# A decoder layer on one core: 44 pairs of the second feed-forward take seven products from sums of weights made during the first feed-forward

## The chip, the cores and the metric

The kernel runs on one core of one Trainium2 chip. The metric is the device time of one execution in microseconds; the time before is the median of three executions, 2144.79 us (2144.66 to 2144.88). One execution was taken by the hardware profiler; it took 2145.35 us, and its traced span is 2143.6 us.

## The reference

One layer in float32 over 16 learned tokens and 256 tokens of 2048 numbers (272 rows): a gated feed-forward at half weight, a mixer (differential attention and a short convolution, gated and merged), a second gated feed-forward at half weight, and a last norm. Cut to what matters here:

```python
def swiglu_ffn(h, w_gu, w_down):
    gate, up = jnp.split(h @ w_gu, 2, axis=-1)
    return (jax.nn.silu(gate) * up) @ w_down

h = rms_norm(s, norm_ffn1[layer])
s = s + 0.5 * swiglu_ffn(h, ffn1_w_gu[layer], ffn1_w_down[layer])
...                                     # the mixer
h = rms_norm(s, norm_ffn2[layer])
s = s + 0.5 * swiglu_ffn(h, ffn2_w_gu[layer], ffn2_w_down[layer])
s = rms_norm(s, norm_final)
return s[:, N_META:]
```

`w_gu` is 2048 x 11264 and `w_down` 5632 x 2048 in both feed-forwards.

## The kernel before

**Numbers.** TensorE multiplies float32 as the sum of a high and a low part. Every weight that arrives from device memory (a tile `st` of up to 1 MB) is therefore split before use: ScalarE casts it to the high part `wh` (L325, L442), VectorE subtracts to get the low part `wl` (L330, L443), and TensorE does three matmuls for each product: high by high, low by high, high by low (L341 to L343, L536 to L538). `wh` and `wl` have three buffers each (`W_BUFS`), `st` has four (`ST_BUFS`). `st` is loaded on SyncE's (SP's) queue (L312, L558).

**First feed-forward** (L716 to L733; roughly the first 800 us). `linear` (L280) multiplies one column group of 512 weights by all 272 rows. It goes over the input in blocks of two chunks of 128 rows of weights: a cast, a subtraction and 2 x 4 x 3 matmuls of 128x272 for each block; one `st` holds two blocks. 11 groups have a gate and an up `linear` of 16 chunks; after six of them and again after the last five, four `linear`s of the down projection run. That is 528 chunks, in 265 blocks (the first chunks come singly). The results of one `linear` are evicted by VectorE and ScalarE during the next (L460 to L466, L193).

**Second feed-forward, gate and up** (`gate_up_mix`, L647; `linear_mix`, L516). 256 tokens and pairs of chunks. A pair forms a 2 x 2 block product of (gate, up) columns by two token halves. A pair of kind D does its eight products, 24 matmuls of 128x512. A pair of kind S does seven, 21 matmuls, from four sums of activations (`Mixed.combine`, L497) and four sums of weights: `t13` (two sums) and `t24` (two sums). The constants `FFN2_FIRST` (the first unit) and `FFN2` (the other ten units) write out the kinds of a unit's eight pairs and, for S, where the sums are made: by VectorE (L570 to L572), or `t13` by two DMAs of 512 KB on GpSimd's (POOL's) queue, the second accumulating (`prefetch`, L576; pairs in the fourth entry, `by_load`), with VectorE adding `t24` (L571, L572). The four blocks in an `st` of 1 MB are split in two tiles for D, and for S in four tiles: `st`'s third block, `st`'s first two, `t24`, `t13` (L596 to L601). `t24` has two buffers (tag `tt`); `t13` uses the three buffers of the pool `aux` (`N_AUX`), which also holds activation sums of other stages.

**What sets the order.** Each engine runs its instructions in one fixed order, and waits at any one of them whose operands are not there. The code is recorded in the order in which it is written; a scheduler then places the instructions on each engine, so a row can stand earlier or later than where the code writes it. The order of the built program is shown below for two engines.

Of the kernel before, what the change touches and what calls it, by code (L numbers as in the profile page):

```python
# [9 lines left out]
F32 = mybir.dt.float32  # L10
# [5 lines left out]
P = 128  # L16
D = 2048
# [3 lines left out]
F = 5632  # L21
# [34 lines left out]
AHEAD = 2  # L56
W_LAST = 8 * GC


@with_exitstack  # L60
def decoder_layer(ctx: ExitStack, tc: tile.TileContext, t, out):
# [5 lines left out]
    aux = ctx.enter_context(tc.tile_pool(name="aux", bufs=N_AUX))  # L67
    tmp = ctx.enter_context(tc.tile_pool(name="tmp", bufs=2))
    psum = ctx.enter_context(tc.tile_pool(name="ps", bufs=8, space=bass.MemoryType.PSUM))

# [192 lines left out]

    pending = []
    last_load, ahead_of_split = [], []
    side = []
# [9 lines left out]
    def drain():  # L276
        while ahead:
            ahead.pop(0)[0]()

    def linear(act, chunks, w, k0, t0, t1, name, evict, before=None, side_at=(5, 9, 13), after=None, later_at=LATER_AT):  # L280
# [11 lines left out]
        for b, b1 in zip(starts, starts[1:] + [len(chunks)]):  # L292
# [41 lines left out]
            for i, c in enumerate(blk):  # L334
                first, last = b + i == 0, b + i == len(chunks) - 1
                for j in range(GC):
                    a, f = acc[j][:, :n], slice(j * P, (j + 1) * P)
                    if 2 * n <= 512:
                        nc.tensor.matmul(acc[j][:, : 2 * n], wh[:, i, f], act.both(c, t0, t1), start=first, stop=False)
                    else:  # L340
                        nc.tensor.matmul(a, wh[:, i, f], act.part(c, 0, t0, t1), start=first, stop=False)  # L341
                        nc.tensor.matmul(a, wh[:, i, f], act.part(c, 1, t0, t1), start=False, stop=False)  # L342
# [131 lines left out]
    class Mixed:  # L474
# [14 lines left out]

        def sum_of_parts(self, p):  # L490
# [4 lines left out]
            self.combine(p, f)  # L495

# [18 lines left out]

    def linear_mix(plan, a, w, name, done, k0=0):  # L516

# [7 lines left out]
        kinds, turn_at, sums_at, by_load = plan  # L525
        nd, ns = kinds.count("D"), kinds.count("S")
        left = {k: 2 * nd * (k in "234x") + ns * (k != "x") for k in "1234567x"}
# [26 lines left out]
        def load(p):  # L554

            st = wpool.tile([P, 4, GW], F32, tag="st", bufs=ST_BUFS, name="st")
            n = 3 if p in by_load else 4
            nc.sync.dma_start(out=st[:, :n, :], in_=w[k0 // 2 + p, :, :n, :])  # L558
            if kinds[p] == "S":
                if not by_load:  # L560
# [19 lines left out]

        far = 2 if by_load else 1
        loaded = {k: load(k) for k in range(far)}
# [29 lines left out]

    def mixed(plan, a, w, name, end):

# [29 lines left out]

        linear_mix(plan, a, w, name, done)

    def gate_up_mix(plan, a, rtok, w_gu, g, m, gi):  # L647
# [11 lines left out]

        mixed(plan, a, w_gu[g], "pg", end)  # L660

# [596 lines left out]
def _laid_out(np, inputs):  # L1258
# [19 lines left out]
    d["w_out"] = np.stack([_in_pairs(np, a["w_out"][0], c, c + GW) for c in (0, W2)])  # L1278
    d["ffn2_w_gu"] = np.stack([_in_pairs(np, a["ffn2_w_gu"][0], c, F + c) for c in range(0, F, GW)])
    w = a["ffn2_w_down"][0]  # L1280
# [3 lines left out]
    return d  # L1284


# [16 lines left out]
```

## Time and profile before

| what | value |
|---|---|
| median of three executions | 2144.79 us |
| the profiled execution | 2145.35 us, span 2143.6 us |
| PE (TensorE) busy | 2132.6 us, 99% of the span |
| DVE (VectorE) busy | 1604.6 us, 75% |
| ACT (ScalarE) busy | 1105.6 us, 52% |
| POOL (GpSimd) busy | 62.6 us, 3% |
| read from device memory | 422.88 MB, 198 GB/s over the span |
| first feed-forward | to about 800 us of the span |
| second feed-forward | from about 1440 us to the end |

Busy times of PE are of pipelined matmuls: one lasts longer than the time until the next starts, and the time between starts is what a matmul costs. "Idle before, releaser" in a group's row tells how long an engine stood before such instructions and what ended that. A DMA's time "to landing" runs from its issue to its completion. Granted clock of TensorE: 0.999 over the span.

### The profile page before, as it was taken

The page shows a single profiled execution, that of the slowest core. Times are in us where ns is not written, and L with a number is a line of the kernel's source. Part 1 is how long each engine was busy: PE and PEld are TensorE (multiplying, and loading weights), DVE is VectorE, ACT ScalarE, POOL GpSimd, SP SyncE. Part 2 cuts the span into 40 slices and gives each one's busy share as a digit, 9 for nine tenths or more (in the row PEclk, how much of TensorE's full clock was granted, in tenths as well). Part 3 has the DMA queues.
Part 4 walks back from the last instruction along what each step waited for, and adds up shares of the span by engine and source line. Part 5 has one row for each costly group of instructions (what it writes and reads, how often), then busy time and mean ns, then how long its engine had stood idle before and what let it go on. Part 6 is the DMA issues. An engine that isn't in the chain of part 4 may idle for free.

```text
span 2143.6 us, 32626 instructions
## 1 busy us (share of the span) xinstructions
PE 2132.6 (99%) x13162; PEld 1925.8 (90%) x13162; DVE 1604.6 (75%) x2113; ACT 1105.6 (52%) x1391; POOL 62.6 (3%) x89
## 2 busy tenths in 40 slices
PE   9999999999999999999999999999999999999998
PEld 9999999999999998899988888888888888888887
DVE  7555554445555668867887889889999899988998
ACT  6444343344333455545555555557665566555665
POOL 0000000000000000000000000000000111001100
PEclk9999999999999999999999999999999999999999
DMA  7554555555545445544355555667876988669853
GB/s 276 179 177 177 179 179 177 177 177 177 177 177 178 177 177 196 182 167 144 138 196 196 197 197 183 214 207 235 252 249 193 276 261 272 216 218 299 261 199 138
DMA packets 69560, 431.29 MB, mean 201 GB/s; under 512 B 8480, under 2 KB 8736, under 8 KB 25888
## 3 DMA queue, kind: packets, MB, share of 16 engines
q1 hardware_dynamic: 57024, 389.72, 51.0%
q0 software_dynamic: 11808, 38.80, 8.3%
q8 instruction: 103, 1.69, 0.3%
q10 hardware_dynamic: 576, 0.67, 0.1%
q14 instruction: 49, 0.40, 0.1%
HBM read 422.88 MB, written 2.10 MB: 198 GB/s over the span
## 4 chain that ended last, share of the span: by engine, by line
PE 99%; DMA 0%; ACT 0%; DVE 0%; issue 0%; ACTq 0%
PE pg L538 6%; PE pg L536 6%; PE pg L537 6%; PE pd L343 4%; PE pg L341 4%; PE pg L342 4%; PE pg L343 4%; PE pd L341 4%; PE pu L343 4%; PE pu L341 4%; PE pu L342 4%; PE pd L342 4%; PE pd L538 4%; PE pd L536 4%; PE pd L537 4%; PE g L538 2%
## 5 line engine op out<-in xcount | busy, mean ns | idle before, releaser
L330 DVE TENSOR_TENSOR wl<-st,wh 128x1024 fp32r<-128x1024 f32 (+1 forms) x329 | 401.0, 1220 | 379.1 <-ACT wh L325 378.9
L325 ACT CAST wh<-st 128x1024 fp32r<-128x1024 f32 (+1 forms) x328 | 343.2, 1047 | 489.3 <-PE pu L342 150.7
L443 DVE TENSOR_TENSOR wl<-st,wh 128x1024 fp32r<-128x1024 f32 (+1 forms) x424 | 470.8, 1118 | 55.3 <-ACT wh L442 52.3
L442 ACT CAST wh<-st 128x1024 fp32r<-128x1024 f32 (+1 forms) x424 | 400.2, 970 | 209.0 <-PE pdx L537 60.4
L442 ACT CAST wh<-t 128x1024 fp32r<-128x1024 f32 x160 | 166.6, 1052 | 242.0 <-DVE t L572 158.9
L443 DVE TENSOR_TENSOR wl<-t,wh 128x1024 fp32r<-128x1024 f32 x160 | 193.8, 1222 | 56.9 <-ACT wh L442 52.3
L341 PE MATMUL pg<-h,wh 128*128 128x272 f32 x704 | 201.9, 288 | 1.6 <-ACT h L206 1.6
L343 PE MATMUL pd<-mh,wl 128*128 128x272 f32 x704 | 203.1, 288 | 0.0
L341 PE MATMUL pd<-mh,wh 128*128 128x272 f32 x704 | 202.2, 287 | 0.0
L341 PE MATMUL pu<-h,wh 128*128 128x272 f32 x704 | 201.9, 287 | 0.0
L342 PE MATMUL pg<-h,wh 128*128 128x272 f32 x704 | 201.8, 288 | 0.0
L343 PE MATMUL pu<-h,wl 128*128 128x272 f32 x704 | 201.7, 287 | 0.0
L342 PE MATMUL pu<-h,wh 128*128 128x272 f32 x704 | 201.7, 286 | 0.0
L342 PE MATMUL pd<-ml,wh 128*128 128x272 f32 x704 | 200.8, 285 | 0.0
L343 PE MATMUL pg<-h,wl 128*128 128x272 f32 x704 | 200.1, 288 | 0.0
L537 PE MATMUL pg<-wh,h 128*128 128x512 f32 x399 | 156.0, 391 | 0.0
L536 PE MATMUL pg<-wh,h 128*128 128x512 f32 x399 | 155.8, 390 | 0.0
L538 PE MATMUL pg<-wl,h 128*128 128x512 f32 x399 | 155.7, 391 | 0.0
L341 PEld LDWEIGHTS pg<-h,wh 128*128 128x128 f32 x704 | 133.1, 190 | 1.9 <-ACT h L206 1.9
L342 PEld LDWEIGHTS pd<-ml,wh 128*128 128x128 f32 x704 | 133.5, 190 | 0.0
L342 PEld LDWEIGHTS pg<-h,wh 128*128 128x128 f32 x704 | 133.1, 190 | 0.0
L342 PEld LDWEIGHTS pu<-h,wh 128*128 128x128 f32 x704 | 132.6, 188 | 0.0
(379 smaller groups left out, 4801.2 us busy)
## 6 DMA issues: line engine op xcount, KB each, us to landing
st<-in_ffn_w_gu_dram SPq DMA_DIRECT2D x140, 1024.0 KB, 4.8
st<-in_ffn_w_down_dram SPq DMA_DIRECT2D x82, 1024.0 KB, 4.8
st<-in_w_in_dram SPq DMA_DIRECT2D x32, 1024.0 KB, 4.8
st<-in_w_gate_dram SPq DMA_DIRECT2D x32, 1024.0 KB, 4.8
t<-in_ffn_w_gu_dram POOLq DMA_DIRECT2D x64, 512.0 KB, 6.7
st<-in_ffn_w_gu_dram SPq DMA_DIRECT2D x32, 768.0 KB, 6.2
st<-in_w_qb_dram SPq DMA_DIRECT2D x16, 1024.0 KB, 4.8
st<-in_w_branch_dram SPq DMA_DIRECT2D x16, 1024.0 KB, 4.8
```

The costliest lines, as they stand in the source:

```text
L325: nc.scalar.copy(out=wh[:, :m, :], in_=sw)
L330: nc.vector.tensor_sub(wl[:, :m, :], sw, wh[:, :m, :].bitcast(F32))
L341: nc.tensor.matmul(a, wh[:, i, f], act.part(c, 0, t0, t1), start=first, stop=False)
L342: nc.tensor.matmul(a, wh[:, i, f], act.part(c, 1, t0, t1), start=False, stop=False)
L343: nc.tensor.matmul(a, wl[:, i, f], act.part(c, 0, t0, t1), start=False, stop=last)
L442: part_last[:] = [nc.scalar.copy(out=wh, in_=src).ins]
L443: part_last.append(nc.vector.tensor_sub(wl, src, wh.bitcast(F32)).ins)
L536: nc.tensor.matmul(ps[k], hi, wh, start=first, stop=False)
L537: nc.tensor.matmul(ps[k], lo, wh, start=False, stop=False)
L538: nc.tensor.matmul(ps[k], hi, wl, start=False, stop=left[k] == 0)
```

## The change

In the second feed-forward a new kind of pair, P, does seven products like S, but its four sums of weights come ready from device memory: `load` brings three blocks of `st` (768 KB), then `t24` and `t13` (512 KB each), all on SP's queue. The first unit goes from five D and three S to four D and four P, the other ten units from four D and four S to three D, four P and one S. So 44 pairs are of kind P, and each of the 11 units has one pair more with seven products. The S that is left has its sums from VectorE; `prefetch` is not used any more.

The sums for P are made by `Making` during the first feed-forward, in 88 halves of 512 KB. Each is a fetch on POOL's queue into a tile `mk` of the pool `aux`, three VectorE adds in place (of 512, 256 and 256 numbers a partition), and a store on POOL's queue into a tensor in device memory, whose pieces are 1 KB long. `tick` is called after each chunk of a `linear` and writes, every fifth time (`TICKS`), the adds and the store of the half two places back (`MAKE_AHEAD`) and the fetch of a new one. The host also lays the blocks of these 44 pairs out a second time (`ffn2_made_of`), without arithmetic. One more sum of activations is made before the second feed-forward.

```diff
-FFN2_FIRST = ("DDDDSSDS", (1,), {(3, 0): 4, (3, 1): 5, (6, 0): 7}, (4, 5))
-FFN2 = ("DDSDSSDS", (1,), {(1, 1): 2, (3, 0): 4, (3, 1): 5, (6, 0): 7}, (2, 4, 5))
+FFN2_FIRST = ("DDDPDPPP", (1,), {}, ())
+FFN2 = ("DDPPDSPP", (1,), {(4, 1): 5}, ())
...
+TICKS = 5
+MAKE_AHEAD = 2
...
+        def fetch(self):
+            self.t = aux.tile([P, 4, GW // 2], F32, tag="act", name="mk")
+            nc.gpsimd.dma_start(out=self.t, in_=t["ffn2_made_of"][self.n, self.k])
+
+        def add(self):
+            v = self.t
+            nc.vector.tensor_add(v[:, 0:2, :], v[:, 0:2, :], v[:, 1:3, :])
+            nc.vector.tensor_add(v[:, 2, :], v[:, 2, :], v[:, 0, :])
+            nc.vector.tensor_add(v[:, 3, :], v[:, 3, :], v[:, 2, :])
+
+        def store(self):
+            if not self.k:
+                made[self.u][self.p] = kept.tile([P, 4, GW], F32, name=f"made{self.u}_{self.p}")
+            cs = slice(self.k * GW // 2, (self.k + 1) * GW // 2)
+            nc.gpsimd.dma_start(out=made[self.u][self.p][:, :, cs], in_=self.t)
...
+    def tick():
+        ticks.append(0)
+        i, k = divmod(len(ticks) - 1, TICKS)
+        if k or i >= len(spare) + MAKE_AHEAD:
+            return
+        if i >= MAKE_AHEAD:
+            spare[i - MAKE_AHEAD].add()
+            spare[i - MAKE_AHEAD].store()
+        if i < len(spare):
+            spare[i].fetch()
...
+                if before is None:
+                    tick()
...
-            n = 3 if p in by_load else 4
+            n = 3 if p in by_load or kinds[p] == "P" else 4
             nc.sync.dma_start(out=st[:, :n, :], in_=w[k0 // 2 + p, :, :n, :])
+            if kinds[p] == "P":
+                t13s[p] = aux.tile([P, 2, GW], F32, tag="act", name="t13")
+                t24s[p] = wpool.tile([P, 2, GW], F32, tag="tt", bufs=2, name="t24")
+                nc.sync.dma_start(out=t24s[p], in_=made[p][:, 2:4, :])
+                nc.sync.dma_start(out=t13s[p], in_=made[p][:, 0:2, :])
...
-                side.append(lambda: hn.sum_of_parts(2))
+                side.append(lambda: [hn.sum_of_parts(2, tmp), hn.sum_of_parts(3)])
...
-                        lambda: [turned(5), hn.sum_of_parts(4)],
-                        lambda: [turned(6), squares(0, 1, 1), hn.sum_of_parts(5)],
+                        lambda: [turned(5), hn.sum_of_parts(5)],
+                        lambda: [turned(6), squares(0, 1, 1), hn.sum_of_parts(6)],
```

In the changed kernel the first feed-forward's subtraction is L373 (L330 before), the adds are L299 to L301, the fetch is L295 and the store L307.

Two places show how the scheduler has put this. The first is VectorE in the first feed-forward, at the start of a `linear` and some blocks on: `wl<-st,wh` is the split of a block; `sg<-pu,sg`, `ml<-sg,mh` and `gt<-pg,rstd` are evictions. Before:

```order
L466 TENSOR_TENSOR sg<-pu_467,sg 128x272
L330 TENSOR_TENSOR wl<-st,wh 128x1024
L193 TENSOR_TENSOR ml_121<-sg,mh_120 128x544 x2
L330 TENSOR_TENSOR wl<-st,wh 128x1024 x7
L460 TENSOR_TENSOR gt<-pg_717,rstd 128x272
```

And now, 36 to 39 blocks into the stage (`mk` is a half being made; L299, L300 and L301 are its three adds, in place):

```order
L373 TENSOR_TENSOR wl<-st,wh 128x1024
L197 TENSOR_TENSOR ml_125<-sg,mh_124 128x544 x2
L301 TENSOR_TENSOR mk<-mk 128x256
L373 TENSOR_TENSOR wl<-st,wh 128x1024
L299 TENSOR_TENSOR mk<-mk 128x512
L300 TENSOR_TENSOR mk<-mk 128x256
L301 TENSOR_TENSOR mk<-mk 128x256
L373 TENSOR_TENSOR wl<-st,wh 128x1024
L299 TENSOR_TENSOR mk<-mk 128x512
L300 TENSOR_TENSOR mk<-mk 128x256
L373 TENSOR_TENSOR wl<-st,wh 128x1024
L301 TENSOR_TENSOR mk<-mk 128x256
```

Where seven splits followed each other, a half's adds now stand in nearly every gap. The code writes one half every 2.5 blocks; in this order the first half's adds stand at the head of the stage, the next three behind the 10th split, the fifth behind the 14th and the 88th, the last, behind the 122nd of 265 splits, so the fifth to the last come at one in 1.3 blocks.

The second place is POOL's queue in the same stage. Before, from the masks at the start to the first DMA that it issues, which belongs to the second feed-forward:

```order
masks.py:197 MEMSET ident 128x128
masks.py:199 ISA
masks.py:199 AFFINE_SELECT ident<-ident 128x128 [waits Pool_49]
L121 AFFINE_SELECT mask<-mask 128x128 [waits DVE_49]
L578 DMA t_14507<-in_ffn_w_gu_dram 128x1024 [waits DVE_49,PE_49]
L579 DMA t_14507<-in_ffn_w_gu_dram 128x1024 [waits DMASW0_49]
```

Now, a piece of the first feed-forward (a wait named DVE is for a half's adds, one named DMASW for an earlier DMA of this queue: a fetch waits until the store from its buffer is through):

```order
L307 DMA made_7_1163<-mk 512x1x256 [waits DMASW2_49,DVE_49]
L307 DMA made_7_1163<-mk 512x1x256 [waits DMASW4_49,DVE_49]
L295 DMA mk<-in_ffn_made_of_dram 128x1024 [waits DMASW5_49]
L295 DMA mk<-in_ffn_made_of_dram 128x1024 [waits DMASW6_49]
L295 DMA mk<-in_ffn_made_of_dram 128x1024 [waits DMASW7_49]
L307 DMA made_2_1333<-mk 512x1x256 [waits DMASW0_49,DVE_49]
L307 DMA made_2_1333<-mk 512x1x256 [waits DMASW1_49,DVE_49]
L295 DMA mk<-in_ffn_made_of_dram 128x1024 [waits DMASW3_49]
L307 DMA made_3_1492<-mk 512x1x256 [waits DMASW2_49,DVE_49]
L295 DMA mk<-in_ffn_made_of_dram 128x1024 [waits DMASW4_49]
```

The queue was empty for two thirds of the program; now it carries 176 DMAs of 512 KB in the first feed-forward, a fetch of a half standing behind the stores of up to two others.

More of the change, by code (lines that the diff above doesn't have):

```diff
@@ L57 @@
 W_LAST = 8 * GC
+TICKS = 5
+MAKE_AHEAD = 2
+MADE = [(u, p) for u in range(F // GW) for p, kind in enumerate((FFN2 if u else FFN2_FIRST)[0]) if kind == "P"]
 @with_exitstack
@@ L68, in decoder_layer @@
     tmp = ctx.enter_context(tc.tile_pool(name="tmp", bufs=2))
+    kept = ctx.enter_context(tc.tile_pool(name="kept", bufs=1, space=bass.MemoryType.DRAM))
     psum = ctx.enter_context(tc.tile_pool(name="ps", bufs=8, space=bass.MemoryType.PSUM))
@@ L264, in decoder_layer @@
     pending = []
+    spare, ticks = [], []
     last_load, ahead_of_split = [], []
@@ L278, in drain, with __init__ @@
             ahead.pop(0)[0]()
+    made = [{} for _ in range(F // GW)]
+    class Making:
+        def __init__(self, n, u, p, k):
+            self.n, self.u, self.p, self.k = n, u, p, k
+        def fetch(self):
[11 more added lines that the diff above has]
+            nc.gpsimd.dma_start(out=made[self.u][self.p][:, :, cs], in_=self.t)
+    for n, (u, p) in enumerate(MADE):
+        spare.extend(Making(n, u, p, k) for k in range(2))
+    def tick():
[8 more added lines that the diff above has]
+            spare[i].fetch()
     def linear(act, chunks, w, k0, t0, t1, name, evict, before=None, side_at=(5, 9, 13), after=None, later_at=LATER_AT):
@@ L488, in sum, with sum_of_parts @@
             self.combine(p, f, pool)
-        def sum_of_parts(self, p):
+        def sum_of_parts(self, p, pool=None):
             f = tmp.tile([P, 2, SEQ], F32, tag="sc", name="mf")
@@ L494, in sum_of_parts @@
             nc.vector.tensor_add(f, hi, lo)
-            self.combine(p, f)
+            self.combine(p, f, pool)
         def combine(self, p, f, pool=None):
@@ L514, in block, with linear_mix @@
             return [self.act.part(c, lo, t0, t0 + P) for lo in range(2)]
-    def linear_mix(plan, a, w, name, done, k0=0):
+    def linear_mix(plan, a, w, name, done, k0=0, made=None):
         kinds, turn_at, sums_at, by_load = plan
-        nd, ns = kinds.count("D"), kinds.count("S")
+        nd = kinds.count("D")
+        ns = len(kinds) - nd
         left = {k: 2 * nd * (k in "234x") + ns * (k != "x") for k in "1234567x"}
@@ L556, in load @@
             st = wpool.tile([P, 4, GW], F32, tag="st", bufs=ST_BUFS, name="st")
-            n = 3 if p in by_load else 4
+            n = 3 if p in by_load or kinds[p] == "P" else 4
             nc.sync.dma_start(out=st[:, :n, :], in_=w[k0 // 2 + p, :, :n, :])
+            if kinds[p] == "P":
[3 more added lines that the diff above has]
+                nc.sync.dma_start(out=t13s[p], in_=made[p][:, 0:2, :])
             if kinds[p] == "S":
-                if not by_load:
+                if not by_load and made is None:
                     t13s[p] = wpool.tile([P, 2, GW], F32, tag="tt", bufs=2, name="t13")
@@ L579, in prefetch @@
             nc.gpsimd.dma_start(out=t13, in_=w[k0 // 2 + p, :, 3:5, :], accum_op=ALU.add)
-        far = 2 if by_load else 1
+        far = 2 if by_load or made is not None else 1
         loaded = {k: load(k) for k in range(far)}
@@ L611, in linear_mix, with mixed @@
                 step(lambda p=p, n=n, products=products: use(p, n, products), src.shape[1] > 1)
-    def mixed(plan, a, w, name, end):
+    def mixed(plan, a, w, name, end, made=None):
         ev = {}
@@ L643, in done @@
                 pending.append(lambda: end(gt, up))
-        linear_mix(plan, a, w, name, done)
+        linear_mix(plan, a, w, name, done, made=made)
     def gate_up_mix(plan, a, rtok, w_gu, g, m, gi):
@@ L658, in end @@
                 later.append(lambda k=k: back(m, 2 * gi + k, up, k))
-        mixed(plan, a, w_gu[g], "pg", end)
+        mixed(plan, a, w_gu[g], "pg", end, made[g])
     def back(act, g, mt, k):
@@ L1279, in _laid_out @@
     d["ffn2_w_gu"] = np.stack([_in_pairs(np, a["ffn2_w_gu"][0], c, F + c) for c in range(0, F, GW)])
+    w = a["ffn2_w_gu"][0]
+    d["ffn2_made_of"] = np.stack(
+        [
+            np.stack([_quarter(w[2 * p * P : 2 * (p + 1) * P], u * GW + k * GW // 2, GW // 2) for k in range(2)])
+            for u, p in MADE
+        ]
+    )
     w = a["ffn2_w_down"][0]
@@ L1284, in _laid_out, with _quarter, _stacked @@
     return d
+def _quarter(rows, c, n):
+    a, b = rows[:P], rows[P:]
+    blocks = [a[:, c : c + n], a[:, F + c : F + c + n], b[:, F + c : F + c + n], b[:, c : c + n]]
+    return _stacked(blocks)
+def _stacked(blocks):
+    import numpy as np
+    return np.stack(blocks, axis=1)
 def kernel(**inputs):
```

## The prediction

> **What bounds the kernel now.** I read the page first, then who waits for whom, then stretches of each stage, and last the operations that the change multiplies or moves.
>
> ```profile
> span 2143.6 us, 32626 instructions
> PE 2132.6 (99%) x13162; PEld 1925.8 (90%) x13162; DVE 1604.6 (75%) x2113; ACT 1105.6 (52%) x1391; POOL 62.6 (3%) x89
> ```
>
> PE is busy all through. A busy PE of pipelined matmuls could hide short stalls, so the table of PE's waits matters more; this is all of it, for the whole span:
>
> ```profile
> PE pg L341 <- ACT h L206: 1.6, 1, 1.6
> PE warm L86 <- DVE ones L80: 1.1, 1, 1.1
> ```
>
> So nothing makes PE wait, and only two things change the time: fewer or more matmuls, and a new wait of PE's. By stage (columns: busy us and count of PE, weight loads, DVE, ACT and POOL, granted clock, DMA share, GB/s), first two stretches of the first feed-forward, then two of the second:
>
> ```profile
> 100.00:300.00 200.00, 200.00 (x1624) 200.00 (x1623) 108.11 (x135) 83.20 (x96) 0.00 (x0) 1.00 0.51 178
> 300.00:500.00 200.00, 200.00 (x1617) 200.00 (x1617) 93.85 (x98) 74.39 (x75) 0.00 (x0) 1.00 0.51 179
> 1500.00:1600.00 100.00, 100.00 (x450) 82.40 (x449) 93.48 (x107) 62.90 (x72) 8.68 (x12) 1.00 0.80 248
> 1900.00:2000.00 100.00, 100.00 (x447) 82.75 (x446) 88.11 (x101) 54.55 (x60) 16.89 (x22) 1.00 0.94 282
> ```
>
> The first feed-forward has DVE half idle, POOL empty and DMA at half share; the second has DVE at some 90% and DMA near full. The change carries work from the second to the first. Whether it fits there is a matter of order, since an engine stops at the first instruction whose data are missing.
>
> **Matmuls removed.** Starts in the second feed-forward, 36 matmuls apart:
>
> ```profile
> 1511.65 0.39 PE L536 MATMUL pg<-wh,h 128*128 128x512 f32 x1
> ...
> 1519.81 0.39 PE L536 MATMUL pgx<-wh,h 128*128 128x512 f32 x1
> ```
>
> 8.16 us / 36 = 0.227 us for one. Each of 11 units turns one pair from 24 to 21 matmuls: 33 x 0.227 = 7.5 us less. PE bounds the stage, so all of it comes off, if nothing new makes PE wait.
>
> **DVE, ACT and DMA in the second feed-forward.** These rows are of two units:
>
> ```profile
> L443 DVE TENSOR_TENSOR wl<-st,wh 128x1024 fp32r<-128x1024 f32 x24 | 29.2, 1218 | 2.1 <-ACT wh L442 2.1
> L443 DVE TENSOR_TENSOR wl<-st,wh 128x512 fp32r<-128x512 f32 x8 | 5.5, 683 | 0.0
> L572 DVE TENSOR_TENSOR t<-t,st 128x512 f32<-128x512 f32 x8 | 5.5, 682 | 0.0
> L571 DVE TENSOR_TENSOR t<-t,st 128x512 f32<-128x512 f32 x8 | 5.5, 682 | 0.0
> L442 ACT CAST wh<-st 128x1024 fp32r<-128x1024 f32 x24 | 25.2, 1052 | 10.5 <-PE pg L537 5.8 <-PE pgx L537 3.7 <-PE pgx L538 0.9
> ```
>
> A unit gets one split of 1024 and one of 512 more (1.22 + 0.68 us) and loses six adds of 512 (L571 and L572 for three pairs, 6 x 0.68): DVE 2.2 us a unit less. ACT has at most two casts of 1.05 us more in the unit's 41 us (180 matmuls x 0.227) and is some 60% busy. Both are covered by PE's work, gain and loss alike: nothing. The extra sum of activations before the stage is some 2.6 us of DVE (two operations of 512 at 0.68, four of 128 at some 0.3) while PE never waits there: nothing, or those 2.6 us once if the cover were gone. DMA: a P brings 1.75 MB as the pairs with accumulating DMAs did, so a unit goes from 10.25 to 11 MB in about 41 us, 281 GB/s in decimal units, what the last stretch above moves already. The second DMA of a POOL pair waited for the first; that goes. Nothing either way, except the wait in the third rival.
>
> **The making, where I expect the loss.** The pace at which the first feed-forward runs, in splits of DVE, with the cast before one of them:
>
> ```profile
> 140.35 1.23 DVE L330 TENSOR_TENSOR wl<-st,wh 128x1024 fp32r<-128x1024 f32 x1 [1.74 <-ACT wh L325]
> ...
> 149.23 1.23 DVE L330 TENSOR_TENSOR wl<-st,wh 128x1024 fp32r<-128x1024 f32 x1 [1.74 <-ACT wh L325]
> ```
>
> ```profile
> 142.23 1.05 ACT L325 CAST wh<-st 128x1024 fp32r<-128x1024 f32 x1 [1.91 <-PE pu L342]
> ```
>
> Three blocks in 8.88 us: 2.96 us a block. The cast waits for PE to let go of a buffer of `wh` from three blocks before; cast and split take 2.3 us from there, and PE needs them two blocks (5.9 us) after. So DVE may be late by 3.6 us before PE stands.
>
> Written one in 2.5 blocks, a half would have 7.4 us. The built order asks for more: 83 halves, the fifth to the last, between the 14th and the 122nd split, 108 blocks x 2.96 = 320 us, 3.85 us a half. There are three `mk` buffers, so a buffer's turn (fetch, adds, store, the next fetch) has 3 x 3.85 = 11.6 us. DVE comes to the adds on that schedule, and if the fetch has not landed, DVE stands, with the splits queued behind, and PE waits for those.
>
> What a turn takes, by the nearest rows. A plain 512 KB load on POOL's queue (its duration, and to landing) and the accumulating load of the same size:
>
> ```profile
> L578 POOL DMA_DIRECT2D t<-in_ffn_w_gu_dram x32: 543/554/702, 1369.3 to 2026.0; - x32
> ...
> DMA to landing us min/median/max: 3.8/6.0/12.0
> ```
>
> ```profile
> L579 POOL DMA_DIRECT2D t<-in_ffn_w_gu_dram x32: 854/883/935, 1373.8 to 2033.7; - x32
> ...
> DMA to landing us min/median/max: 5.4/8.2/10.3
> ```
>
> and a store of 512 KB on SP's queue, and the slowest kind of POOL's DMAs:
>
> ```profile
> out_dram<-sT SPq DMA_DIRECT2D x2, 512.0 KB, 3.0
> sT<-dpb POOLq DMA_DIRECT2D x8, 256.0 KB, 10.7
> ```
>
> - Fetch: 6.0 us, L578's median; it is the same transfer on the same queue beside weight loads. Bounds 3.8 (its minimum) and 8.2.
> - Adds: 0.68 for 512 numbers; I take 0.42 for 256, an estimate from 0.68 less 256 numbers at the rate between the rows of 512 and 1024 (1218 - 683 = 535 ns for 512, so 0.27). 0.68 + 2 x 0.42 = 1.5 us, with one split of 1.2 us between them by the order: 2.7.
> - Store: between 3.0 (SP's, long pieces) and 10.7. Nearest is L578 again, but a store is cut into 512 pieces of 1 KB instead of 128 of 4 KB. I add 1.0, between nothing and the 1.7 by which L578's own 0.55 on POOL would grow fourfold: 7.0.
> - POOL's queue: two issues of other buffers stand ahead of a DMA, 2 x 0.55 = 1.1 us a turn.
>
> The sum is 6.0 + 2.7 + 7.0 + 1.1 = 16.8 us a turn, 5.6 us a half, against 3.85: 1.75 x 83 = 145 us, less the 3.6 that DVE may be late: 142 us. It is not given back: after the 122nd split PE has no slack to catch up with.
>
> A second limit agrees with the sign but is small. At 3.85 us a half moves 1.05 MB and the weights of 1.3 blocks 0.68 MB: 449 GB/s. A busy stretch of the second feed-forward, 1650 to 1670 us in slices of half a microsecond, tops out at 442:
>
> ```profile
> GB/s 197 393 360 442 442 16 49 180 213 377 426 410 229 266 209 197 201 217 197 197 197 180 209 254 270 295 381 393 397 381 279 393 393 426 344 197 33 0 0 0
> ```
>
> So the pace asked for is more than the DMA engines give even at their best, by 2%, some 5 us; at 5.6 us a half it is 309 GB/s, a tenth above the busiest stretch quoted. The turn of the buffers limits first.
>
> **Sum.** The profiled execution took 2145.35 us, 1.75 more than its span and 0.56 more than the median. -7.5 + 142 = +134 us: 2279.5 on the profiled execution, 2279 on the median.
>
> **Rivals.**
> 1. The buffers keep up, and the change is faster. If a fetch and a store together take less than 11.6 - 2.7 - 1.1 = 7.8 us, DVE never waits beyond its slack, and only the 33 matmuls count: 2144.8 - 7.5 = 2137.3. For it: L578's minimum 3.8 and the SP store's 3.0 give 6.8, and DMA in the first feed-forward is at 0.51, not 0.8 to 0.94. Against it: L578's median, the extra traffic itself, and the 442 GB/s. Chance 0.09, and 0.02 that a loss of 4 to 12 us cancels the gain. The Trainium skill (DMA: Bandwidth & Descriptors, Anatomy of one DMA — SWDGE (gpsimd) path) gives 2.0 us and the bytes at 436 GB/s for one DMA of this queue, 3.2 us for 512 KB; by that rule a fetch and a store take 6.4 us and this rival holds. This trace disagrees: L578's fastest of 32 is 3.8 us and its median 6.0.
> 2. The making hurts more: many short pieces to device memory make DMAs crowd each other. With a fetch of 8.2 and a store of 10.7 a turn is 22.7 us, a half 7.6: 3.7 x 83 = 309 us, and 2144.8 + 309 - 3.6 - 7.5 = 2442. Chance 0.07. For it the DMAs of small pieces at 10.7 us; against it that those accumulate.
> 3. SP's queue in the second feed-forward: `t24` of a unit's last pair may be loaded only when the S pair two before has let go of its buffer, and the next unit's loads stand behind it. It has two pairs of 21 matmuls, 9.5 us, for a 512 KB load; only if loads took over 9.5 us would PE wait, by some 4 us a unit, 10 x 4 = 40 us, on top of the forecast: 2319, inside its range. Chance 0.05, taken from the forecast's. Against it: a 1 MB load lands in 4.8 us by its median (`st<-in_ffn_w_gu_dram`).
>
> ```profile
> st<-in_ffn_w_gu_dram SPq DMA_DIRECT2D x140, 1024.0 KB, 4.8
> ```
>
> **How the numbers follow.** Forecast, PE held up by the making: 0.82, with the third rival within it. Its own range: fetch 4.9 and store 5.5 (half way to the bounds) give a turn of 14.2, +73 - 3.6 - 7.5 = +62, 2207; fetch 7.2 and store 9.0 give 20.0, +234 - 11 = +223, 2368. Range 2200 to 2370; left out are rival 1, rival 2 and little else, 0.2. What a measurement of this kernel can tell from no change is about 0.2%, 4.3 us. Faster by over that 0.09 (rival 1), within it 0.02, slower 0.89.
>
> **What would show it.** Right: DVE's waits name a DMA of `mk` at L299 with over 100 us; PE's waits name `wl` L373, all before some 520 us of the span; the last `mk` add stands near 500 us (the 14th split at about 45, plus 83 x 5.6); L295 lands in 6 us and L307 in 7; PE's second feed-forward is 7 to 8 us shorter and has no waits. Wrong: no wait at L299, or waits of PE at L582 to L584, or PE waiting in the first feed-forward for something other than `wl`.

## The result and the profile after

The changed kernel takes 2323.22 us (median of five executions, 2321.48 to 2330.27) against 2144.82 us: a ratio of 1.0841, 95% interval 1.082 to 1.0862. The profiled execution took 2321.48 us, 176.1 us more than that of before. Forecast were 2279 us and a range of 2200 to 2370: the side and the place were right, the size was 44 us short.

First the page after, its span, PE's share, and PE's busy share and granted clock in 40 slices of 58 us:

```profile
span 2319.5 us, 33283 instructions
PE 2186.8 (94%) x13129; PEld 1972.3 (85%) x13129; DVE 1700.9 (73%) x2338; ACT 1121.8 (48%) x1414; POOL 128.3 (6%) x201
...
PE   9687777778999999999999999999999999999998
...
PEclk9898888889999999999999999999999999999999
```

PE makes 33 matmuls fewer and is busy 54 us longer. The first ten slices, 580 us, are thin in both rows; behind them both rows read 9, as before (PE's last slice reads 8 in both kernels). PE's waits after, all but one of 0.4 us:

```profile
PE pu L386 <- DVE wl L373: 43.4, 10, 6.6
PE pg L386 <- DVE wl L373: 42.4, 12, 5.8
PE pd L386 <- DVE wl L373: 32.7, 10, 5.8
PE pg L385 <- DVE h L211: 2.5, 1, 2.5
PE pg L384 <- ACT h L210: 1.5, 1, 1.5
PE warm L90 <- DVE ones L84: 1.1, 1, 1.1
```

118.5 us of waiting for the low parts of weights, and no wait in the second feed-forward. The stretch in which the halves are made, and one behind it (columns as in the prediction):

```profile
45.00:546.00 501.00, 382.43 (x2626) 375.02 (x2625) 275.85 (x452) 133.69 (x149) 104.53 (x165) 0.87 0.82 290
...
600.00:700.00 100.00, 100.00 (x812) 100.00 (x812) 50.80 (x61) 40.77 (x45) 0.00 (x0) 1.00 0.51 179
```

The same stretch of before, for the count:

```profile
45.00:546.00 501.00, 501.00 (x4058) 501.00 (x4057) 256.19 (x297) 198.32 (x218) 0.00 (x0) 1.00 0.51 179
```

4058 matmuls before, 2626 after: 1432 x 0.1235 us (501 / 4058) = 177 us lost in this stretch. PE's account of the 501 us is 119 us idle and some 58 us by which 2626 matmuls took longer than at 0.1235 each, at a granted clock of 0.87. That account says where PE was, not what set the length. To see what did, take DVE's groups in the same 501 us (busy and mean, then idle before and who ended it):

```profile
L373 DVE TENSOR_TENSOR wl<-st,wh 128x1024 fp32r<-128x1024 f32 x109 | 132.0, 1218 | 0.4 <-ACT wh L368 0.4
L299 DVE TENSOR_TENSOR mk<-mk 128x512 f32<-128x512 f32 x83 | 56.7, 689 | 221.9 <-DMA mk<-in_ffn_made_of_dram 221.9
```

In the same stretch of before the splits read:

```profile
L330 DVE TENSOR_TENSOR wl<-st,wh 128x1024 fp32r<-128x1024 f32 x170 | 208.3, 1225 | 240.1 <-ACT wh L325 240.1
```

Before, a split waited for its cast, and that for PE: 240 us in all, the mark of a stage bound by PE. After, splits wait 0.4 us and the adds wait 222 us for their fetch. DVE never stood for PE, so PE's lower clock cannot have set the length; it only made PE late in time that it had to stand through anyway. 109 splits instead of 170 are 61 blocks x 2.96 = 181 us. And POOL in that stretch:

```profile
L307 POOL DMA_DIRECT2D made<-mk x83 | 60.3, 730 | 120.1 <-DVE mk L301 102.1 <-DVE mk L300 13.6 <-DVE rsa L263 1.5
L295 POOL DMA_DIRECT2D mk<-in_ffn_made_of_dram x82 | 45.8, 559 | 270.2 <-DMA made<-mk 269.8 <-issue 0.2
```

Issues, waits of fetches for a store to land and waits of stores for the adds fill 496 of POOL's 501 us. So the queue was in use as one closed loop: fetch, adds, store, fetch. The operations' own rows (duration in ns, first and last start; then the time to landing):

```profile
L299 DVE TENSOR_TENSOR mk<-mk x88: 677/691/696, 7.6 to 546.1; 128x512 f32<-128x512 f32 x88
```

```profile
mk<-in_ffn_made_of_dram POOLq DMA_DIRECT2D x88, 512.0 KB, 6.5
made<-mk POOLq DMA_DIRECT2D x88, 512.0 KB, 6.8
```

The fifth half's adds start at 46.7 us and the last's at 546.1: 499.4 / 83 = 6.02 us a half, a turn of 18.1 us for a buffer, where 16.8 was forecast.

### The profile page after: what moved, and what is told of

It is laid out like the page before. It is cut to its first block, busy times and chain, and to the rows that moved or that the text cites. A ratio compares the mean times of both kernels' runs of the same rounds, so it can differ in the third digit from the quotient of the medians.

```text
span 2319.5 us, 33283 instructions
## 1 busy us (share of the span) xinstructions
PE 2186.8 (94%) x13129; PEld 1972.3 (85%) x13129; DVE 1700.9 (73%) x2338; ACT 1121.8 (48%) x1414; POOL 128.3 (6%) x201
## 4 chain that ended last, share of the span: by engine, by line
PE 76%; DMA 9%; issue 8%; DVE 5%; POOL 1%; ACT 0%; SPq 0%; DVEq 0%; POOLq 0%; ACTq 0%
DMA mk<-in_ffn_made_of_dram 6%; PE pg L584 6%; PE pg L582 6%; PE pg L583 6%; PE pd L584 3%; PE pd L582 3%; PE pd L583 3%; PE pd L386 3%; PE pd L384 3%; PE pd L385 3%; PE g L584 2%; PE g L583 2%; PE g L582 2%; PE pg L386 2%; PE pg L384 2%
## 5 line engine op out<-in xcount | busy, mean ns | idle before, releaser
L373 DVE TENSOR_TENSOR wl<-st,wh 128x1024 fp32r<-128x1024 f32 (+1 forms) x329 | 399.5, 1218 | 228.6 <-ACT wh L368 228.4
L487 ACT CAST wh<-t 128x1024 fp32r<-128x1024 f32 x182 | 189.7, 1052 | 219.2 <-DVE t L623 148.7
L488 DVE TENSOR_TENSOR wl<-t,wh 128x1024 fp32r<-128x1024 f32 x182 | 220.0, 1222 | 66.2 <-ACT wh L487 62.2
L299 DVE TENSOR_TENSOR mk<-mk 128x512 f32<-128x512 f32 x88 | 60.1, 689 | 228.2 <-DMA mk<-in_ffn_made_of_dram 228.2
L385 PE MATMUL pg<-h,wh 128*128 128x272 f32 x704 | 210.2, 300 | 2.5 <-DVE h L211 2.5
L384 PE MATMUL pg<-h,wh 128*128 128x272 f32 x704 | 210.5, 301 | 1.5 <-ACT h L210 1.5
L384 PE MATMUL pu<-h,wh 128*128 128x272 f32 x704 | 209.7, 298 | 0.4 <-DVE norm L238 0.4
L385 PE MATMUL pu<-h,wh 128*128 128x272 f32 x704 | 209.0, 297 | 0.0
L386 PEld LDWEIGHTS pg<-h,wl 128*128 128x128 f32 x704 | 141.3, 202 | 46.1 <-DVE wl L373 46.1
L386 PEld LDWEIGHTS pu<-h,wl 128*128 128x128 f32 x704 | 140.6, 200 | 45.6 <-DVE wl L373 45.6
L386 PEld LDWEIGHTS pd<-mh,wl 128*128 128x128 f32 x704 | 138.8, 197 | 34.9 <-DVE wl L373 34.9
L385 PEld LDWEIGHTS pg<-h,wh 128*128 128x128 f32 x704 | 141.9, 202 | 2.8 <-DVE h L211 2.8
L384 PEld LDWEIGHTS pg<-h,wh 128*128 128x128 f32 x704 | 142.3, 203 | 1.8 <-ACT h L210 1.8
L582 PE MATMUL pg<-wh,h 128*128 128x512 f32 x366 | 143.3, 392 | 0.0
```

Of the source, the lines that this page charges most:

```text
L299: nc.vector.tensor_add(v[:, 0:2, :], v[:, 0:2, :], v[:, 1:3, :])
L373: nc.vector.tensor_sub(wl[:, :m, :], sw, wh[:, :m, :].bitcast(F32))
L487: part_last[:] = [nc.scalar.copy(out=wh, in_=src).ins]
L488: part_last.append(nc.vector.tensor_sub(wl, src, wh.bitcast(F32)).ins)
L582: nc.tensor.matmul(ps[k], hi, wh, start=first, stop=False)
```

## The experiments

The theory: the built order asks for a half in every 1.3 blocks, and three buffers with their fetches and stores on one queue cannot follow. Against it stood: the seven-product pairs bring nothing; the DMA engines are full; the lower clock of TensorE, by the traffic or by the idle time, is the loss; POOL's queue alone is.

**1. The gain by itself.** `tick` is taken out, and the pairs P load raw blocks in place of the sums. Left out is the making, so the products of these pairs are of other numbers.

```diff
-                if before is None:
-                    tick()
...
-                nc.sync.dma_start(out=t24s[p], in_=made[p][:, 2:4, :])
-                nc.sync.dma_start(out=t13s[p], in_=made[p][:, 0:2, :])
+                nc.sync.dma_start(out=t24s[p], in_=w[k0 // 2 + p, :, 2:4, :])
+                nc.sync.dma_start(out=t13s[p], in_=w[k0 // 2 + p, :, 0:2, :])
```

> Nothing is made in the first feed-forward: no fetches, adds or stores; the pairs of kind P load t24 and t13 as two 512 KB pieces of the raw weights (the same sizes on the same queue), so their products are of other numbers. Theory A (the whole loss lies in the making, because VectorE waits in its fixed order for fetches whose buffers come round too slowly; the second feed-forward gets its 33 matmuls for nothing): 2144.8 - 7.5 = 2137.3 us, no wait of PE's anywhere beyond those at the start, clock 1.00. Rival B (part of the loss is in the second feed-forward, at the loads on SP's queue that wait for the buffers of t24): above 2141, with PE waits at L582 to L584.

Measured: 2137.82 us (2137.53 to 2138.01) against 2144.77, ratio 0.9967, 0.9954 to 0.9979. That is 7.0 us less where 33 matmuls of 0.227 are 7.5. A stretch of its second feed-forward:

```profile
1900.00:2000.00 100.00, 100.00 (x447) 82.79 (x446) 85.33 (x93) 58.61 (x65) 7.65 (x10) 1.00 0.88 293
```

PE is busy for all of it. The gain is there, and the making costs some 184 us (2321.5 less 2137.8).

**2. The adds held to their place.** An order edge ties a half's adds behind the split that the code has just written, which gives one half in 2.5 blocks, 7.4 us.

```diff
+            with tc.issue_after(split_last[0]):
-            nc.vector.tensor_add(v[:, 0:2, :], v[:, 0:2, :], v[:, 1:3, :])
+                nc.vector.tensor_add(v[:, 0:2, :], v[:, 0:2, :], v[:, 1:3, :])
...
-                nc.vector.tensor_sub(wl[:, :m, :], sw, wh[:, :m, :].bitcast(F32))
+                split_last[:] = [nc.vector.tensor_sub(wl[:, :m, :], sw, wh[:, :m, :].bitcast(F32)).ins]
```

> The full change, and the three adds of a half may not stand ahead of the split of the block after which the code writes them (an order edge on VectorE), so a half comes every 2.5 blocks, 7.4 us, and a buffer's turn may take 22.2 us; nothing else differs. Theory A: a turn needs 17 to 18 us (fetch 6.5, store 6.8 as measured in the changed kernel, adds, queue), so VectorE never stands longer than its slack, the making is free and the time is 2137.3 us, the clock 1.00 throughout. Rival C (the DMA engines are the limit: the changed kernel's first stage moved no more than 304 GB/s in any 100 us while 1.05 MB a half beside 179 GB/s are asked here, 320 GB/s): the stage of 640 us gets at least 5% longer, 2137 + 33 = 2170 or more. Rival D (88 x 1.5 us of adds on VectorE are the cost, wherever they stand): above 2200. Rival E (the DMA traffic or the busier VectorE lowers TensorE's granted clock): clock below 0.97 over the first 650 us and 2150 or more.

Measured: 2163.86 us (2153.1 to 2178.8), ratio 1.0092, 1.0059 to 1.0125, where 2137.3 was expected. Most of the loss is gone, but not all, so the pace by itself is not the whole cause: at 7.4 us a half the turn of three buffers would be 22 us, and DVE still waits. Its waits, and POOL's, in the profiled execution, which took 2178.8 us:

```profile
POOL mk L296 <- DMA made<-mk: 549.8, 85, 11.8
DVE mk L301 <- DMA mk<-in_ffn_made_of_dram: 133.5, 57, 7.6
```

A piece of POOL's queue shows why (start, duration, what; in brackets the idle time before and what ended it):

```profile
402.95 0.54 POOL L296 DMA_DIRECT2D mk<-in_ffn_made_of_dram  x1 [8.05 <-DMA made<-mk]
403.58 0.73 POOL L309 DMA_DIRECT2D made<-mk  x1
409.43 0.54 POOL L296 DMA_DIRECT2D mk<-in_ffn_made_of_dram  x1 [5.12 <-DMA made<-mk]
410.06 0.73 POOL L309 DMA_DIRECT2D made<-mk  x1
```

A fetch stands until the store just issued ahead of it has landed, and the next store, of another buffer and long ready, stands behind that fetch. So only one store is under way at a time: from the end of a half's adds to the start of its store 8.1 us pass on the mean (fifth to 85th half), against 0.4 in experiment 5 below. The scheduler had put each fetch one place ahead of the store that the code writes before it.

**3. The DMAs without the adds.** The changed kernel with `.add()` taken out. Every half is fetched and stored as it is, so all DMAs and all bytes stay, and the pairs P get raw blocks in place of the sums:

```diff
-            spare[i - MAKE_AHEAD].add()
```

> The changed kernel without the three adds: every half is fetched and stored as it is, so the same 92 MB move on POOL's queue as fast as three buffers and the queue let them, VectorE has no part in it, and the pairs of kind P multiply raw weights. Theory A: nothing that PE needs waits for POOL's DMAs; weight loads land later than 4.8 us but within the four buffers' 23 us; 2137 to 2140 us, clock 1.00, while the stores' waits stay on POOL. Rival C (DMA engines saturated by the making): PE waits in the first 500 us and 2160 us or more.

Measured: 2146.67 us, between the two expectations. (Experiments 3, 4 and 7 to 11 are one execution each.) The first 100 us, and a stretch behind:

```profile
0.00:100.00 100.00, 91.80 (x692) 88.79 (x693) 61.29 (x92) 52.11 (x78) 22.56 (x41) 1.00 0.98 382
```

```profile
300.00:400.00 100.00, 100.00 (x809) 100.00 (x808) 46.77 (x48) 36.03 (x36) 23.71 (x37) 1.00 1.00 377
```

In the second stretch the DMA engines are at a share of 1.00, and PE does not notice: what the full engines delay is the halves (a fetch lands in 9.0 us by the median, 6.5 in the changed kernel), which no other engine waits for here. The first 100 us of experiment 1, for comparison:

```profile
0.00:100.00 100.00, 96.68 (x759) 95.52 (x760) 64.26 (x95) 54.49 (x80) 0.99 (x7) 1.00 0.63 230
```

67 matmuls fewer, 8 us, are nearly all of the 9 us above 2137.8: there the first weights share the engines with the first fetches. Behind them, full engines alone are not the loss, and their traffic does not lower the clock (1.00).

**4. Idle time and the clock.** The kernel before, with 33 operations of VectorE of 9.2 us each, one behind every fourth split, and no DMA added (`tick` is called after each chunk, as in the changed kernel).

```diff
+    def tick():
+        ticks.append(0)
+        if len(ticks) % 8 == 1 and len(ticks) <= 264:
+            with tc.issue_after(split_last[0]):
+                nc.vector.tensor_reduce(out=busy, in_=ones.unsqueeze(1).to_broadcast([P, 68, P]), axis=AX.X, op=ALU.max)
...
```

> The kernel before, without the change, with 33 VectorE reductions of 8704 numbers a partition (9.1 us each by 8704/960 and the slope between the rows of 512 and 1024) put behind every fourth split of the first feed-forward: VectorE is late by 9.1 - 1.7 us of gap - 3.6 us of slack = 3.8 us, 33 times, 125 us of PE idle in all, with no extra DMA. Theory F (PE's idle stretches of 3 to 7 us lower its granted clock for some microseconds after each, and in the changed kernel this added to the waits): the clock of the stage falls to 0.85 to 0.93 as in the changed kernel, and the loss is more than the idle, 160 us and more. Rival E (traffic or VectorE's activity lowers the clock): clock 0.99 to 1.00, loss 125 us or less.

Measured: 2292.46 us, 147.7 us lost, between the two expectations. PE's waits and a stretch:

```profile
PE pg L352 <- DVE wl L339: 33.1, 10, 4.8
PE pu L352 <- DVE wl L339: 33.0, 11, 4.3
PE pd L352 <- DVE wl L339: 29.9, 11, 4.0
PE ssq_ps L232 <- DVE norm L227: 6.4, 1, 6.4
```

```profile
200.00:300.00 100.00, 81.79 (x595) 80.49 (x594) 92.74 (x51) 30.36 (x33) 0.00 (x0) 0.91 0.34 127
```

102.4 us of waits and some 45 us of slower matmuls make up the 147.7 us, with DMA at a share of 0.34 and the clock at 0.91: idle time lowers the clock here, and no traffic is needed for it. VectorE, 93% busy in this stretch, is not the reason either: in the kernel before it is as busy from 1500 to 1600 us, at a clock of 1.00. This too is an account of where PE was. How much of the 45 us set the length is not shown: VectorE was busy for 463 of the 501 us from 45 to 546, and its splits waited for casts, and so for PE, for 37.8 us:

```profile
L339 DVE TENSOR_TENSOR wl<-st,wh 128x1024 fp32r<-128x1024 f32 x123 | 146.0, 1218 | 37.8 <-ACT wh L334 37.7
```

In the changed kernel the lower clock is seen after a wait:

```profile
321.45 0.60 PE L386 MATMUL pu<-h,wl 128*128 128x272 f32 x1 [3.77 <-DVE wl L373]
321.85 0.43 PE L384 MATMUL pu<-h,wh 128*128 128x272 f32 x1
322.08 0.43 PE L385 MATMUL pu<-h,wh 128*128 128x272 f32 x1
...
324.67 0.29 PE L385 MATMUL pu<-h,wh 128*128 128x272 f32 x1
324.79 0.29 PE L386 MATMUL pu<-h,wl 128*128 128x272 f32 x1
```

Starts 0.23 us apart for 2.9 us, then 0.12. The Trainium skill (TensorE: Matmul & The Clock Gate, Part 1: The HAM clock gate) gives this as a rule: half clock after an idle window of about 3.4 us, full clock again after about as long of work. The trace agrees in kind; the half rate lasted 2.9 us here and some 5.8 us behind one stall of this experiment. One would count the 58 us of slower matmuls in the account above as a part of the change's loss. DVE's groups there speak against that: splits waited 0.4 us in all for their casts. A run that keeps PE's clock up in the changed kernel was not tried.

**5. Both engines held to their place.** Beside the edge of experiment 2, a fetch is issued behind the store that the code writes ahead of it.

```diff
-            nc.gpsimd.dma_start(out=self.t, in_=t["ffn2_made_of"][self.n, self.k])
+            with ExitStack() as order:
+                for ins in store_last:
+                    order.enter_context(tc.issue_after(ins))
+                nc.gpsimd.dma_start(out=self.t, in_=t["ffn2_made_of"][self.n, self.k])
...
-            nc.gpsimd.dma_start(out=made[self.u][self.p][:, :, cs], in_=self.t)
+            store_last[:] = [nc.gpsimd.dma_start(out=made[self.u][self.p][:, :, cs], in_=self.t).ins]
```

> As the pinned kernel with a half every 2.5 blocks, and on POOL's queue each fetch may not stand ahead of the store that the code writes before it (an order edge on GpSimd). Theory G (what was left of the loss, 26 us, is POOL's queue: there a fetch waits 6.5 us for the last store to land with the next store, whose adds are done, queued behind it, so stores follow each other at no less than 7.5 to 8 us, more than the 7.4 us of the pace): stores now go out when their adds are done, a fetch has 14.8 us less 3 us for 6.5 us, VectorE does not wait for it, 2138 us plus at most 5 us at the start, where the first fetches run beside the first loads. Rival H (the fetches are late because 16 DMA engines are shared with the weight loads): the same bytes at the same pace, so 2150 to 2180 us as without this edge.

Measured: 2140.74 us (2140.22 to 2141.57), ratio 0.9982, 0.9973 to 0.9991. DVE's wait, of 133.5 us in experiment 2:

```profile
DVE mk L305 <- DMA mk<-in_ffn_made_of_dram: 10.6, 7, 4.1
```

The same making in the same stage now costs 3 us. Nothing but the order differs from the changed kernel; with it the adds are spread further, to 692 us of the span where they ended at 550.

**6. A later start.** The first two fetches each wait for a one-element write of VectorE, the first behind the tenth split at 28.8 us, so that the first weights come alone.

```diff
+            if not store_last:
+                with tc.issue_after(split_last[0]):
+                    nc.vector.memset(self.t[:, 0, 0:1], 0.0)
```

> As the kernel with both order edges, and the first two fetches wait for a memset of one element of their tile on VectorE behind the 9th split, so that they do not run beside the first loads (there PE lost some 8 us when POOL's DMAs ran at once, and 2 us in the kernel before). Theory G with a start cost: 2137.8 us, the time of the gain alone, and 3 to 5 us less than the run without the late start. Rival H: 2150 us or more. If the start costs nothing, both are equal.

Measured: 2138.41 us (2137.92 to 2139.0), ratio 0.997, 0.9959 to 0.9982. The stretch of the making:

```profile
45.00:546.00 501.00, 501.00 (x4058) 501.00 (x4057) 350.15 (x500) 198.80 (x218) 85.74 (x136) 1.00 0.89 320
```

4058 matmuls, as many as before, with the sums made beside them. This version beats both kernels, by 0.3% and by 8%.

**7. The queue alone.** The edge on POOL without the one on DVE: the adds stay packed, a half in 1.34 blocks. Against experiment 5:

```diff
-            with tc.issue_after(split_last[0]):
-                nc.vector.tensor_add(v[:, 0:2, :], v[:, 0:2, :], v[:, 1:3, :])
+            nc.vector.tensor_add(v[:, 0:2, :], v[:, 0:2, :], v[:, 1:3, :])
...
```

> The changed kernel with the order edge on POOL's queue alone; VectorE's order is left to the scheduler, which again puts the halves at one in 1.34 blocks, 3.98 us. Theory A and G together: three buffers need 1.5 of adds + 0.7 + 6.8 store + 0.7 + 6.5 fetch = 16.2 us a turn, 5.4 us a half, so VectorE is held (5.4 - 3.98) x 85 = 121 us, and with the lower clock (1.45 us lost for 1 us of idle, as the run without the change showed) some 175 us: 2300 us, hardly better than the 2323 of the change. Rival (POOL's queue alone is the cause, and VectorE's order harmless): 2140 to 2150 us.

Measured: 2299.76 us. DVE's wait:

```profile
DVE mk L303 <- DMA mk<-in_ffn_made_of_dram: 208.7, 66, 6.7
```

By the trace two things gain the 23 us here (2323.2 to 2299.8). A buffer's mean turn went from 18.1 to 17.7 us, which over 83 halves is some 11 us, and the order asks for 1.34 blocks a half in place of 1.3, which is as much again. Between experiments 2 and 5 the queue's order is worth 23 us (2163.9 to 2140.7, though the executions of experiment 2 lie up to 26 us apart). The rest hangs on the pace: 17.7 / 3 is 5.9 us a half where 3.98 was asked. That the expected 2300 us was met is luck. It came from a turn of 16.2 us, too short, and 54 us for the lower clock; from 45 to 546 us no split waited for its cast, so nothing shows that the clock added to the time.

**8. Both held, at 1.5 blocks.** Experiment 5 with one half in three chunks.

```diff
-TICKS = 5
+TICKS = 3
```

> Both order edges and a half written every 3 chunks instead of 5: 1.5 blocks, 4.44 us. Theory A with a turn of 16.2 us: (5.4 - 4.44) x 87 = 84 us held, 120 us with the lower clock, 2258 us, clock under 0.95 in the first 450 us. Rival (with both queues in order the making is free at any pace the engines can carry, and 1.05 MB in 4.44 us beside the weights is 413 GB/s or less, at which the run without adds had no wait of PE's): 2140 us.

Measured: 2257.81 us. The adds' row, and DVE's wait:

```profile
L305 DVE TENSOR_TENSOR mk<-mk x88: 678/693/695, 42.0 to 545.4; 128x512 f32<-128x512 f32 x88
```

```profile
DVE mk L305 <- DMA mk<-in_ffn_made_of_dram: 184.4, 65, 6.8
```

503.4 us for 87 halves are 5.79 us, where 4.44 (1.5 x 2.96) was asked: 1.35 x 87 = 117 us, and 117.1 lie between this run and experiment 5. At a fixed and orderly pace, pace against turn accounts for the whole of the loss. The expected 2258 us was met by the same luck as in experiment 7: 84 us by a turn of 16.2, the rest by the clock. The turn is 17.4 (3 x 5.79), and splits waited 0.6 us for casts:

```profile
L379 DVE TENSOR_TENSOR wl<-st,wh 128x1024 fp32r<-128x1024 f32 x130 | 156.5, 1217 | 0.6 <-ACT wh L374 0.6
```

**9, 10 and 11. Buffers, and the point where it turns.** Five buffers of `mk` need the room of one buffer of `st`; run 9 is the control that only takes that one away from experiment 8, run 10 gives it to `mk` and fetches a half one place earlier, run 11 is experiment 5 with `TICKS` at 4, one half in 2 blocks, 5.92 us. Runs 9 (the first change) and 10 (all three) against experiment 8:

```diff
-ST_BUFS = 4
+ST_BUFS = 3
...
-N_AUX = 3
+N_AUX = 5
...
-MAKE_AHEAD = 2
+MAKE_AHEAD = 3
```

> The kernel with adds and fetches both held to their place at one half in 1.5 blocks (2257.8 us) with three buffers of st instead of four; three buffers of mk stay. It is the control for the next run, which needs that memory. Theory (the turn of the three mk buffers sets the loss): unchanged but for what the missing st buffer costs, 2255 to 2270 us; DVE waits for mk some 180 us. Rival (st is what is short): well over 2270 with waits of ACT for st in the first feed-forward.

> The same with five buffers of mk instead of three, and each half fetched three places ahead instead of two. Theory: a turn of some 16 to 18 us divided by five buffers is 3.2 to 3.6 us a half, under the 4.44 us that the order asks for, so the loss goes: 2137 to 2150 us, DVE's waits for mk under 20 us, granted clock 0.99 or more. Rival (a queue of POOL that lets one store pass at a time, or DMA capacity, sets the loss): the waits for mk stay over 100 us and the time over 2220 us.

> Adds and fetches both held to their place, three buffers of mk and four of st, one half in 2 blocks: 5.92 us a half. Theory: three buffers give a half in some 5.4 to 6.0 us, just enough: 2139 to 2160 us, waits of DVE for mk under 50 us. Rival (the loss grows evenly with the pace, no threshold): half way between 2140.7 at 2.5 blocks and 2257.8 at 1.5 blocks, some 2199 us.

Measured: 2257.05, 2172.84 and 2147.39 us. In run 9 nothing changed. In run 10 five buffers take away 84 of 117 us, so the buffers' turn did set the pace, but it missed what I expected by 23 us. Its adds, and stretches of 100 us:

```profile
L305 DVE TENSOR_TENSOR mk<-mk x88: 676/687/694, 46.6 to 465.2; 128x512 f32<-128x512 f32 x88
```

```profile
100.00:200.00 100.00, 96.47 (x765) 95.60 (x764) 77.43 (x123) 38.53 (x44) 26.54 (x43) 1.00 0.99 381
200.00:300.00 100.00, 95.32 (x761) 94.01 (x760) 77.15 (x123) 37.75 (x44) 26.06 (x42) 1.00 0.99 390
```

418.6 / 87 = 4.81 us a half, still over 4.44, at a DMA share of 0.99. A half and the weights of 1.5 blocks are 1.835 MB; in 4.81 us that is 381 GB/s, what the rows show. So the second limit took over where the first was moved away: the DMA engines. In run 11, DVE's wait:

```profile
DVE mk L305 <- DMA mk<-in_ffn_made_of_dram: 84.9, 54, 5.4
```

84.9 us of waits, more than the 50 expected, cost only 6.7 us over experiment 5; by the theory most of them stay within what DVE may be late. A buffer's mean turn is 17.9 us, 5.98 a half, where 5.92 was asked. So the loss does not grow evenly with the pace: over experiment 5 it is 7 us at 2 blocks and 117 at 1.5.

## Why the prediction was right, and where its size was off

- **33 matmuls, -7.5 us.** Right: 7.0 us less in experiment 1, 6.4 with the making in experiment 6.
- **The second feed-forward otherwise nothing.** Right: PE has no wait there after. The third rival, `t24` held up by its buffers on SP's queue, did not come.
- **The making, +142 us.** Right in cause and place, too small: 2321.48 - 2145.35 + 7.5 = 183.6 us. Its terms: the pace asked for holds, since holding the adds back removes most of the loss and both edges nearly all. A buffer's turn, from the starts and landings in the trace for the fifth half on, is 18.1 us on the mean: fetch 6.3 (6.0 in the sum), store 6.5 (7.0), first to last add 3.2 (2.7), and 2.05 for the rest, where the sum had 1.1. These 2.05 are 0.5 us from a landing to the first add, 1.1 from the last add to the store, and 0.5 from the store's landing to the next fetch. The step that fell most short is "POOL's queue: two issues of other buffers stand ahead of a DMA, 2 x 0.55 = 1.1 us a turn". It priced what stands ahead as issues, but what stands ahead also waits: a store stands behind a fetch that waits for another store to land. (Most of the 269.8 us of such waits is the landing itself, which the turn counts as store.) In experiment 7, where no fetch is put ahead of a ready store, the last add to the store takes 0.4 us and not 1.1. With 6.02 us a half the prediction's own formula gives (6.02 - 3.85) x 83 - 3.6 = 177 us, which is also what the stretch from 45 to 546 us lost. Another 4 us lie ahead of it, in the first 45 us, where PE made 275 matmuls and before 309 (34 x 0.1235). Most of that is the first weights sharing the engines with the first fetches: with the adds at their place, experiment 5 made 290 matmuls there with early fetches and experiment 6 made 313 with late ones. Together 181 of 183.6.

The two rows of that start, of before and then of after:

```profile
0.00:45.00 45.00, 42.38 (x309) 42.01 (x310) 34.41 (x60) 32.40 (x55) 0.99 (x7) 1.00 0.77 284
```

```profile
0.00:45.00 45.00, 39.29 (x275) 37.95 (x276) 35.74 (x64) 28.64 (x49) 7.20 (x17) 1.00 0.94 353
```

- **The range.** The store is said to go half way to its bounds, but from 7.0 that is 5.0 and 8.85, not 5.5 and 9.0. With 5.0 the lower end is some 2193 in place of 2207; the measured time lies inside either way.
- **The second limit, some 5 us.** Too small: it divided by the best half microsecond, 442 GB/s, but over 100 us at a share of 0.99 to 1.00 the engines gave 377 to 390. At 381 the 1.73 MB of a half and 1.3 blocks take 4.54 us, which over 83 halves is 0.69 x 83 = 57 us, an estimate. It lay hidden under the turn. The Trainium skill (DMA: Bandwidth & Descriptors, Where 436 GB/s comes from) puts the limit of device memory at about 358 GB/s for one core, half of what two cores share, and that of the ports into on-chip memory at 435. The rows, with reads and writes in them, lie between, so here the lower figure did not hold them back.
- **Rival 1, the buffers keep up.** It needed a fetch and a store in 7.8 us together, and they took 12.8. So it fell by the turn, and experiment 10 shows that it would have fallen by the second limit as well at this pace. Its fetch of 3.2 us by the fit of the Trainium skill (DMA: Bandwidth & Descriptors, Anatomy of one DMA — SWDGE (gpsimd) path) is not reached: the fastest of 88 took 3.7 us, the median 6.5.
- **Rival 2, DMAs crowding each other to 8.2 and 10.7 us.** Not in the changed kernel. With five buffers landings of about that size come (10.2 and 9.2 us), with the engines at a share of 0.99; whether the short pieces have a part in that was not tried.
- **What would show it.** Waits at L299 over 100 us (228), PE's waits naming `wl` L373, landings of 6 and 7 us: right. The last add, expected near 500 us, stood at 546, and so did PE's last wait, expected before some 520, both by the longer turn.

## What to carry to other kernels

Work that is to fill an engine's gaps has a pace given by the built order, not by the written one: read the order, and divide a buffer's whole turn by the number of buffers before asking whether it fits. On an in-order queue, look at what each waiting instruction holds up behind it; the same 176 DMAs cost some 184 us in one order and 3 us in another. Behind the first limit find the second, from a sustained rate and not from a peak.

## What the runs showed of the hardware

- TensorE's rate is halved for 3 to 6 us behind a long stall (0.227 in place of 0.123 us a matmul of 272 columns). Behind the first 10 us of the changed kernel this followed all 12 stalls of 4.3 us or more, 4 of 11 between 3.3 and 4.3, and none that was shorter. Whether it lengthens the kernel depends on who sets the pace: splits waited 37.8 us for casts in experiment 4, and 0.4 in the changed kernel.
- The DMA engines of this core at a share of 0.99 to 1.00 moved 377 to 390 GB/s over 100 us, with weight loads still in time for PE in experiment 3 behind its first 100 us: a 1 MB load landed there in 7.4 us by the median, against 5.4 in the changed kernel.

```profile
st<-in_ffn_w_gu_dram SPq DMA_DIRECT2D x128, 1024.0 KB, 7.4
```
